# Wider exp tiles and single score and output banks in a planned attention kernel

The change gives ScalarE's exp three PSUM banks at a time instead of two, pays for them with one of VectorE's two score banks and one of the two output banks, shortens VectorE's chains from ten cells to six, and lets the steps of two chains mix.

## The chip, the cores and the metric

The kernel runs on one core of a Trainium2 chip. The metric is device time in microseconds, median of several executions. An execution can fall in a slower state, seen by a lower clock granted to TensorE.

TensorE does the matmuls, ScalarE and VectorE work on their results, and GpSimd does some of the arithmetic beside them. PSUM is the memory that TensorE writes to; this program uses it as eight banks, each of which holds one block of scores or of outputs. SBUF is the core's working memory.

## The reference

```python
batch, n_q_heads, n_kv_heads, seq, head_dim = (8, 8, 2, 1024, 64)
...
scores = scale * np.matmul(q_group, k_group.transpose(0, 1, 3, 2))
scores_max = np.max(scores, axis=-1, keepdims=True)
attn = np.exp(scores - scores_max)
attn = attn / (np.sum(attn, axis=-1, keepdims=True) + 1e-08)
output[:, q_start:q_end, :, :] = np.matmul(attn, v_group)
```

There are 64 heads. Each head is cut into two halves of queries, so there are 128 jobs, and each job has eight cells. A cell is a 128x512 block of scores: 128 keys by 512 queries.

## The kernel before

For each cell TensorE makes a score block in a PSUM bank (one matmul), an exp is taken of it, and TensorE multiplies the result with V (four small matmuls). After eight cells VectorE normalises the job's output. The exp is taken in one of two ways. ScalarE does two cells at a time from a two-bank tile. VectorE converts single cells from banks of their own ("p1", a conversion to an integer that is nearly the bits of the exponential) and then repairs ten of them at a time by a chain: a mask, a linear factor on GpSimd, a product and a sum.

What makes this kernel special is that the order of all this is fixed before launch. A Python function, the planner, walks through the program with assumed durations, always takes the operation that can start first, and writes down a list. Every engine then executes its part of the list in order. In the code, `pe` and `dve` are the times at which TensorE and VectorE come free, `ready` holds the times at which exps are done, `obank_free` the times at which the output banks come free, and `at` is the earliest start of an operation. "qk" is a score matmul, "pv" the output matmuls of a cell, "norm" a normalisation. The parts that matter here:

```python
A_CELLS, D_BANKS, O_BANKS = (2, 2), 2, 2
GROUP, PARTS = 10, 2
# ... in the planner's loop:
        for i, s in enumerate(open_jobs):
            for c in rem[s]:
                at = max(pe, FIRST_PV, ready.get(s * nkc + c, INF))
                if at < INF:
                    best = min(best or (INF,), (at, 3 + i, "pv", (s, c)))
        if len(open_jobs) < O_BANKS and next_job < nj:
            at = min(ready.get(next_job * nkc + c, INF) for c in range(nkc))
            at = max(pe, FIRST_PV, min(obank_free), at)
            if at < INF:
                best = min(best or (INF,), (at, 3 + len(open_jobs), "open", next_job))
# ... cut
        elif kind == "open":
            o = first_free(obank_free)
            obank[arg] = o
            obank_free[o] = INF
            open_jobs.append(arg)
# ... cut
        elif kind == "pv":
            # ... cut
            pe = t + PV
        elif kind == "norm":
            # ... cut
            dve = t + NORM
            obank_free[obank[s]] = dve + FROM_DVE
```

And what the list drives:

```python
    def output_mms(s, cell, opens, closes, bk):
        if opens:
            ops_of[s] = obanks[bk].tile([128, NQS, E1], FP32, name=f"ops{bk}")
        for qs in range(NQS):
            nc.tensor.matmul(ops_of[s][:, qs, :], ...)   # cut
    def normalise(s):
        o = ops_of.pop(s)
        nc.vector.reciprocal(out=rec, in_=o[:, :, D])
        nc.vector.tensor_tensor(out=stage[(b, h)][:, :, side, :], in0=o[:, :, 0:D],
            in1=rec.unsqueeze(2).to_broadcast([128, NQS, D]), op=ALU.mult)
```

The softmax here doesn't subtract the row's maximum and nothing guards it: scores larger than these inputs give would overflow.

Of the kernel before, what the change touches and what calls it, by code (L numbers as in the profile page):

```python
# [11 lines left out]

CURVE_A, CURVE_B = 0.32988085, -0.33401025

A_CELLS, D_BANKS, O_BANKS = (2, 2), 2, 2
GROUP, PARTS = 10, 2
CHAIN = ("and", "line", "prod", "add")
ON_POOL = ("line",)

# [6 lines left out]
def make_plan(nj, nkc):  # L26
# [6 lines left out]

    QK, PV, P1, NORM = 0.216, 0.1225, 0.603, 0.555
    EXP = (0.05, 0.4268)
    FOUR, TWO, POOL_ONE = (0.20, 0.133), (0.16, 0.27), (0.25, 0.43)
    COST = {"and": FOUR, "line": POOL_ONE, "prod": TWO, "add": TWO}
    FROM_PE, FROM_PV, FROM_ACT, FROM_DVE, FROM_POOL = 0.21, 0.16, 0.165, 0.10, 0.15
    LIVE_A, LIVE_D, PENDING, PER_JOB, LEAD, RAMP, AHEAD, FIRST_PV = 28, 5, 16, 2, 6, 6, 0.04, 2.0
    INF = 1e9  # L40
    FIRST_TURN, FIRST_LOAD, EACH_LOAD = 3.3, 4.5, 4.2
    ops = []
    pe = act = dve = 0.0
    a_free, bank, obank_free = [0.0] * len(A_CELLS), [0.0] * D_BANKS, [0.0] * O_BANKS
    todo = [list(range(nkc)) for _ in range(nj)]
    taken = [0] * nj
# [19 lines left out]
    while normed < nj:  # L66
# [3 lines left out]
        lead = min(LEAD, job_a // RAMP)  # L70
        job_d = max(job_d, job_a + lead)
        while job_d < nj and (
            taken[job_d] >= PER_JOB or not todo[job_d]
        ):
            job_d += 1
        if job_a < nj:
# [7 lines left out]
        if job_d < nj and job_d <= job_a + lead + 1 and pending < PENDING:  # L84
            if cur or live["D"] < LIVE_D:
                t = max(pe, min(bank), loaded(job_d))
                if t < INF:
                    best = min(best or (INF,), (t, 2, "qk", 1, t))
        for i, s in enumerate(open_jobs):
            for c in rem[s]:  # L90
                at = max(pe, FIRST_PV, ready.get(s * nkc + c, INF))
# [2 lines left out]
        if len(open_jobs) < O_BANKS and next_job < nj:  # L94
            at = min(ready.get(next_job * nkc + c, INF) for c in range(nkc))
            at = max(pe, FIRST_PV, min(obank_free), at)
            if at < INF:
                best = min(best or (INF,), (at, 3 + len(open_jobs), "open", next_job))
        for q, p, kind in ((normq, 0, "norm"), (p1q, 1, "p1"), (chainq, 2, "chain")):
            if q:  # L100
                at = q[0][0]
                if kind != "chain" or CHAIN[q[0][3]] not in ON_POOL:
                    at = max(dve, at)
                best = min(best or (INF,), (at, p, kind, 0))
        if cur and job_d >= nj and not p1q:
            best = min(best or (INF,), (dve, 9, "flush", 0))
        t, _, kind, arg = best[:4]
        if kind == "qk":
            t = best[4]
            pe = t + QK  # L110
            j = job_d if arg else job_a
            cell = j * nkc + todo[j].pop(0)
            if not arg:
                if open_a is None:
                    slot = first_free(a_free)
                    a_id += 1
                    live["A"] += 1
                    open_a = {"slot": slot, "t": a_free[slot], "cells": []}
                    a_free[slot] = INF
                o = open_a  # L120
                ops.append((t, "qk", cell, "A", a_id, o["slot"], len(o["cells"])))
                o["cells"].append(cell)
                home[cell] = ("A", a_id)
                if len(o["cells"]) == A_CELLS[o["slot"]] or not any(todo[job_a:]):
                    act = max(act, pe + FROM_PE)
                    ops.append((act, "exp", a_id, tuple(o["cells"])))
                    act += EXP[0] + EXP[1] * len(o["cells"])
                    a_free[o["slot"]] = act + FROM_ACT
                    uses[("A", a_id)] = len(o["cells"])
                    for x in o["cells"]:  # L130
                        ready[x] = act + FROM_ACT
                    open_a = None
            else:
                taken[j] += 1
                k = first_free(bank)
                bank[k] = INF
                pending += 1
                ops.append((t, "qk", cell, "D", k, 0, 0))
                p1q.append((pe + FROM_PE, cell, k))
# [5 lines that stand above are left out]
            rem[arg] = list(range(nkc))  # L145
            next_job += 1
        elif kind == "pv":
            s, c = arg
            cell = s * nkc + c
            opens = len(rem[s]) == nkc  # L150
            rem[s].remove(c)
            done = not rem[s]
            ops.append((t, "pv", s, cell, opens, done, obank[s]))
            pe = t + PV
            h = home[cell]
            uses[h] -= 1
            if not uses[h]:
                live[h[0]] -= 1
            if done:
                open_jobs.remove(s)  # L160
                normq.append((pe + FROM_PV, s))
        elif kind == "norm":
            s = normq.pop(0)[1]
            ops.append((t, "norm", s))
            dve = t + NORM
            obank_free[obank[s]] = dve + FROM_DVE
            normed += 1
        elif kind == "p1":
            _, cell, k = p1q.pop(0)
            if not cur:  # L170
                d_id += 1
                live["D"] += 1
            ops.append((t, "p1", cell, k, d_id, len(cur)))
            dve = t + P1
            bank[k] = dve + FROM_DVE
            cur.append(cell)
            home[cell] = ("D", d_id)
            if len(cur) == GROUP:
                chainq.append((dve, d_id, cur, 0))
                cur = []  # L180
        elif kind == "flush":
            chainq.append((dve, d_id, cur, 0))
            cur = []
        else:
            _, g, cells, step = chainq.pop(0)
            ops.append((t, "chain", g, len(cells), CHAIN[step]))
            name = CHAIN[step]
            fixed, each = COST[name.rstrip("0123456789")]
            end = t + fixed + each * len(cells[part(name, len(cells))])
            dve = end if name not in ON_POOL else dve  # L190
            if step + 1 < len(CHAIN):
                at = end
                if (name in ON_POOL) != (CHAIN[step + 1] in ON_POOL):
                    at += FROM_POOL if name in ON_POOL else FROM_DVE
                chainq.insert(0, (at, g, cells, step + 1))
            else:
                pending -= len(cells)
                uses[("D", g)] = len(cells)
                for x in cells:
                    ready[x] = dve + FROM_DVE  # L200
# [4 lines left out]
def kernel(  # L205
# [27 lines left out]
    PIECE = 512  # L233
    WARM = 30
    CAST_GAP = 3.0
    P_TILES = 28
    POOL_DMA = 1.0
    OBSERVE = 8
    scale = 1.0 / math.sqrt(D)
    bits_scale = 128.0 * scale * math.log2(math.e)  # L240
    bits_bias = 128.0 * 127.0
# [30 lines left out]
            for i in range(n)  # L272
        ]

    apools, dbanks, obanks = psum_pools("aps", 2), psum_pools("dps", 2), psum_pools("ops", 2)

    p_ring = const_pool.tile([128, P_TILES, 2, QBS], BF16)
    blank = const_pool.tile([128, 128], BF16)
    nc.vector.memset(blank, 1.0)  # L279
    ident = const_pool.tile([128, 128], BF16)  # L280
# [75 lines left out]
    def first_loads():  # L356
# [5 lines left out]

        hk = first_pool.tile([128, NHC, 3, D], BF16, name="hk")

        tk = [
            dbanks[0].tile([128, HALF], BF16, name="dps0"),
            apools[1].tile([128, HALF], BF16, name="aps1"),
        ]
        lo, hi = slice(0, D), slice(D, 2 * D)

        def turn_k(w, half, bank):
# [21 lines left out]
        for two in range(2):  # L393
            place_v(0, 0, two)

        warm = obanks[1].tile([128, 128], FP32, name="ops1")

        def keep_warm(n):
            for _ in range(n):
# [1 line left out]
            return mm.ins  # L401

        hq = first_pool.tile([128, NHC, 2 * D], BF16, name="hq")
        tq = [
            dbanks[1].tile([128, HALF], BF16, name="dps1"),
            obanks[0].tile([128, HALF], BF16, name="ops0"),
        ]
        qT[(0, 0)] = qT_pool.tile([128, HALF], BF16, name="qT")
        last_score[0] = keep_warm(WARM)
        for n, half in enumerate(halves):  # L410
# [15 lines left out]
            else:  # L426
                nc.vector.tensor_copy(out=qT[(0, 0)][:, cols], in_=tq[n][:, cols])  # L427
                nc.scalar.copy(out=ksets[0][lo, 0, 0, :HALF][:, cols], in_=tk[n][lo, cols])
        nc.scalar.copy(out=qT[(0, 0)][:, : HALF // 2], in_=tq[0][:, : HALF // 2])
        turn_k(1, slice(0, NHC), 0)  # L430
        last_score[0] = keep_warm(4)
        put_k(0, 1, slice(0, NHC), 0)
        nc.gpsimd.dma_start(out=ksets[0][hi, 0, 1, :], in_=ksets[0][lo, 0, 0, :])  # L433

    p_of = {}
    psum = {}
# [6 lines left out]
    def score(cell, kind, n, slot, col):  # L443
        b, h, side = jobs[cell // NKC]
        c = cell % NKC
        if kind == "A":
            if col == 0:
                psum[("A", n)] = apools[slot].tile([128, 2, QBS], FP32, name=f"aps{slot}")
            dst = psum[("A", n)][:, col, :]
        else:  # L450
            dst = psum[cell] = dbanks[n].tile([128, QBS], FP32, name=f"dps{n}")
# [8 lines left out]
    def exps(n, cells):  # L460
# [4 lines left out]
        )  # L465

        exp_ins.append(act.ins)
        if n >= P_TILES and n % OBSERVE == 0:
            seen = exp_ins[n - P_TILES + OBSERVE - 1]
            tc.add_manual_dep(act.ins, seen.name, SYNC, reason="ring")  # L470
        for col, cell in enumerate(cells):
# [15 lines left out]
    def exp_curve(g, m, step):  # L487
# [4 lines left out]
            temps[g] = z, y  # L492
        cells = part(step, m)
        pd, z, y = groups[g][:, cells], temps[g][0][:, cells], temps[g][1][:, cells]
        if step.startswith("and"):
            eng.tensor_scalar(  # L496
                out=z, in0=pd, scalar1=0x7F, scalar2=None, op0=ALU.bitwise_and
            )
# [136 lines left out]
```

## Time and profile before

| | before |
|---|---|
| time, median of 3 runs | 386.97 us |
| span of the profile | 384.9 us |
| ScalarE busy | 375.1 us, 97% |
| TensorE busy | 368.1 us, 96% (matmul records overlap) |
| VectorE busy | 350.1 us, 91% |
| exps | 406 of two cells |
| VectorE's cells | 212 of 1024 |

Records of one engine overlap: an exp's record is 1100 ns long on average, but the next one starts 918 ns after it. So work is best counted in pitches, the differences of start times. The lines themselves stand in the prediction; in them PEld is TensorE's loading of weights, DVE is VectorE, ACT is ScalarE and POOL is GpSimd.

### The profile page before, as it was taken

The page shows a single profiled execution, that of the slowest core. Times are in us where ns is not written, and L with a number is a line of the kernel's source. Part 1 is how long each engine was busy: PE and PEld are TensorE (multiplying, and loading weights), DVE is VectorE, ACT ScalarE, POOL GpSimd, SP SyncE. Part 2 cuts the span into 40 slices and gives each one's busy share as a digit, 9 for nine tenths or more (in the row PEclk, how much of TensorE's full clock was granted, in tenths as well). Part 3 has the DMA queues.
Part 4 walks back from the last instruction along what each step waited for, and adds up shares of the span by engine and source line. Part 5 has one row for each costly group of instructions (what it writes and reads, how often), then busy time and mean ns, then how long its engine had stood idle before and what let it go on. Part 6 is the DMA issues. An engine that isn't in the chain of part 4 may idle for free.

```text
span 384.9 us, 12057 instructions
## 1 busy us (share of the span) xinstructions
PE 368.1 (96%) x5172; PEld 234.5 (61%) x5172; DVE 350.1 (91%) x544; ACT 375.1 (97%) x411; POOL 165.3 (43%) x147
## 2 busy tenths in 40 slices
PE   8879999999999999999999999999999999999985
PEld 6425565656666666666666565666566566666654
DVE  4879999999999999999999999999999999999692
ACT  5999999999999999999999999999999999999994
POOL 5394571716246171625535252535445261531410
PEclk9999999999999999999999999999999999999998
DMA  8888979597859769595865949486584756621213
GB/s 137 152 130 141 141 138 173 113 129 148 128 111 134 132 109 141 123 138 85 151 123 126 125 90 169 74 150 113 119 143 109 111 100 113 109 70 29 71 43 83
DMA packets 102422, 45.49 MB, mean 118 GB/s; under 512 B 63776, under 2 KB 100896, under 8 KB 101120
## 3 DMA queue, kind: packets, MB, share of 16 engines
q1 hardware_dynamic: 82096, 31.21, 37.5%
q0 software_dynamic: 19728, 13.25, 29.8%
q8 instruction: 40, 0.66, 0.8%
q10 hardware_dynamic: 544, 0.26, 0.2%
q14 instruction: 14, 0.11, 0.1%
HBM read 25.17 MB, written 27.00 MB: 136 GB/s over the span
## 4 chain that ended last, share of the span: by engine, by line
ACT 94%; PE 2%; DMA 1%; issue 1%; DVE 0%; SPq 0%; POOLq 0%
ACT p_ring L463 94%; PE ops L522 1%; PE aps L452 1%; DMA fk<-in_k_dram 1%; DMA kset<-kset 1%; SPq L389 0%; DVE ost L538 0%; ACT hk L411 0%; DVE kset L382 0%; DVE qT L427 0%; PE aps L373 0%; DVE rec L535 0%; PE ops L419 0%; PE ops L400 0%; POOLq L433 0%
## 5 line engine op out<-in xcount | busy, mean ns | idle before, releaser
L463 ACT ACTIVATE p_ring<-aps 128x1024 bf16<-128x1024 f32 x406 | 372.4, 1100 | 1.2 <-PE aps L452 1.2
L452 PE MATMUL aps<-qT,kset 128*128 128x512 bf16 x812 | 240.6, 378 | 11.4 <-ACT p_ring L463 8.8
L522 PEld LDWEIGHTS <-p_ring 128*128 128x128 bf16 x3248 | 137.5, 97 | 60.4 <-ACT p_ring L463 0.2
L522 PE MATMUL ops<-vset,p_ring 128*128 128x65 bf16 x3248 | 150.8, 194 | 0.1
L477 DVE TENSOR_SCALAR pd<-dps 128x512 uint16<-128x512 f32 x212 | 138.0, 682 | 13.2 <-PE dps L452 12.3
L500 POOL TENSOR_SCALAR y<-z 128x5120 f16<-128x5120 uint16 (+1 forms) x22 | 94.6, 4301 | 82.7 <-DVE rec L535 45.0
L452 PEld LDWEIGHTS <-kset 128*128 128x128 bf16 x1024 | 82.6, 97 | 58.8 <-issue 26.7
L314 POOL DMA_DIRECT2D scr_q<-in_q_dram x63 | 34.7, 551 | 99.0 <-PE aps L452 47.6
L452 PE MATMUL dps<-qT,kset 128*128 128x512 bf16 x212 | 73.4, 378 | 0.0
L511 DVE TENSOR_TENSOR pd<-pd,y 128x5120 uint16<-128x5120 uint16 (+1 forms) x22 | 59.8, 2719 | 0.1
L509 DVE TENSOR_TENSOR y<-z,y 128x5120 f16<-128x5120 uint16 (+1 forms) x22 | 59.8, 2718 | 0.0
L538 DVE TENSOR_TENSOR ost<-ops,rec 128x256 f32<-128x256 f32 x128 | 54.3, 424 | 4.4
L522 PEld LDWEIGHTS <-pd 128*128 128x128 bf16 x848 | 41.3, 98 | 25.6 <-DVE pd L511 3.6
L522 PE MATMUL ops<-vset,pd 128*128 128x65 bf16 x848 | 48.4, 194 | 0.0
L496 DVE TENSOR_SCALAR z<-pd 128x5120 uint16<-128x5120 uint16 (+1 forms) x22 | 31.7, 1443 | 0.6
L535 DVE RECIPROCAL rec<-ops 128x4 f32<-128x4 f32 x128 | 22.5, 176 | 9.8 <-PE ops L522 8.8
L347 POOL DMA_DIRECT2D vset<-in_v_dram x32 | 24.9, 782 | 0.0
L314 POOL DMA_DIRECT2D scr_k<-in_k_dram x15 | 7.8, 521 | 24.1 <-PE aps L452 16.7
L400 PE MATMUL ops<-blank 128*128 128x128 bf16 x40 | 4.4, 286 | 1.1 <-DVE blank L279 1.1
L400 PEld LDWEIGHTS <-blank 128*128 128x128 bf16 x40 | 3.8, 135 | 1.1 <-DVE blank L279 1.1
L354 POOL DMA_DIRECT2D kset<-kset x6 | 3.2, 537 | 0.0
L411 ACT ACT_TABLE_LOAD x1 | 1.3, 1283 | 1.8 <-issue 1.8
(23 smaller groups left out, 8.7 us busy)
## 6 DMA issues: line engine op xcount, KB each, us to landing
out_dram<-ost SPq DMA_DIRECT2D x63, 256.0 KB, 2.9
scr_q<-in_q_dram POOLq DMA_DIRECT2D x63, 128.0 KB, 3.6
kset<-kT SPq DMA_DIRECT2D x60, 64.0 KB, 3.1
vset<-in_v_dram POOLq DMA_DIRECT2D x32, 64.0 KB, 4.0
scr_k<-in_k_dram POOLq DMA_DIRECT2D x15, 128.0 KB, 3.2
qT<-scr_q SPq DMA_TRANSPOSE x63, 4.0
kset<-kset POOLq DMA_DIRECT2D x7, 128.0 KB, 4.0
fq<-in_q_dram ACTq DMA_DIRECT2D x2, 128.0 KB, 3.2
```

Of the source, the lines that this page charges most:

```text
L314: dma = nc.gpsimd.dma_start(out=scr.rearrange("(p f) -> p f", f=1024), in_=src.rearrange("(p s) d -> p (s d)", s=1024 // D),)
L347: nc.gpsimd.dma_start(out=vsets[b % 2][:, g, two * NHC : (two + 1) * NHC, 0:D], in_=v[b, g].rearrange("(c p two) d -> two p c d", p=128, t ...
L452: last_score[0] = nc.tensor.matmul(dst, lhsT=ksets[b % 2][:, h // HPG, side, c * 128 : (c + 1) * 128], rhs=qT[(b, h)], start=True, stop=Tr ...
L463: act = nc.scalar.activation(out=pt[:, 0:m], in_=psum.pop(("A", n))[:, 0:m], func=AF.Exp, scale=scale)
L477: nc.vector.tensor_scalar(out=groups[g][:, slot], in0=psum.pop(cell), scalar1=bits_scale, scalar2=bits_bias, op0=ALU.mult, op1=ALU.add,)
L496: eng.tensor_scalar(out=z, in0=pd, scalar1=0x7F, scalar2=None, op0=ALU.bitwise_and)
L500: eng.tensor_scalar(out=y, in0=z, scalar1=CURVE_A / 128.0, scalar2=CURVE_B, op0=ALU.mult, op1=ALU.add,)
L509: eng.tensor_tensor(out=y, in0=z, in1=y, op=ALU.mult)
L511: eng.tensor_tensor(out=pd, in0=pd, in1=y, op=ALU.add)
L522: nc.tensor.matmul(ops_of[s][:, qs, :], lhsT=p_of[cell][:, qs * 128 : (qs + 1) * 128], rhs=vsets[b % 2][:, h // HPG, c, :], start=opens an ...
L535: nc.vector.reciprocal(out=rec, in_=o[:, :, D])
L538: nc.vector.tensor_tensor(out=stage[(b, h)][:, :, side, :], in0=o[:, :, 0:D], in1=rec.unsqueeze(2).to_broadcast([128, NQS, D]), op=ALU.mult,)
```

## The change

The intent: an exp of 1536 elements pays the fixed cost of an instruction once for three cells. The eight banks become 3 + 3 for ScalarE, one for VectorE's scores and one for outputs. Shorter chains finish sooner; the planner now keeps GpSimd's linear factor and VectorE's chain steps apart in time. The core of the diff:

```diff
-A_CELLS, D_BANKS, O_BANKS = (2, 2), 2, 2
-GROUP, PARTS = 10, 2
+A_CELLS, D_BANKS, O_BANKS = (3, 3), 1, 1
+GROUP, PARTS = 6, 2
...
-    FOUR, TWO, POOL_ONE = (0.20, 0.133), (0.16, 0.27), (0.25, 0.43)
+    FOUR, TWO, POOL_ONE = (0.09, 0.133), (0.05, 0.27), (0.25, 0.43)
...
-    LIVE_A, LIVE_D, PENDING, PER_JOB, LEAD, RAMP, AHEAD, FIRST_PV = 28, 5, 16, 2, 6, 6, 0.04, 2.0
+    LIVE_A, LIVE_D, PENDING, PER_JOB, LEAD, RAMP, AHEAD, FIRST_PV = 18, 5, 12, 2, 6, 6, 0, 2.0
...
+        for i, (at, _, _, step) in enumerate(chainq):
+            if CHAIN[step] in ON_POOL:
+                at = max(at, pool, two_end)
+            else:
+                at = max(at, dve, pool)
+            best = min(best or (INF,), (at, 2 + i, "chain", i))
...
-    P_TILES = 28
+    P_TILES = 18
...
-    OBSERVE = 8
+    OBSERVE = 16
...
+        nc.scalar.dma_start(
+            out=ksets[0][hi, 0, 1, :HALF], in_=ksets[0][lo, 0, 0, :HALF]
+        )
```

More of the change, by code (lines that the diff above doesn't have):

```diff
@@ L35, in make_plan @@
     EXP = (0.05, 0.4268)
-    FOUR, TWO, POOL_ONE = (0.20, 0.133), (0.16, 0.27), (0.25, 0.43)
+    FOUR, TWO, POOL_ONE = (0.09, 0.133), (0.05, 0.27), (0.25, 0.43)
     COST = {"and": FOUR, "line": POOL_ONE, "prod": TWO, "add": TWO}
     FROM_PE, FROM_PV, FROM_ACT, FROM_DVE, FROM_POOL = 0.21, 0.16, 0.165, 0.10, 0.15
-    LIVE_A, LIVE_D, PENDING, PER_JOB, LEAD, RAMP, AHEAD, FIRST_PV = 28, 5, 16, 2, 6, 6, 0.04, 2.0
+    LIVE_A, LIVE_D, PENDING, PER_JOB, LEAD, RAMP, AHEAD, FIRST_PV = 18, 5, 12, 2, 6, 6, 0, 2.0
     INF = 1e9
-    FIRST_TURN, FIRST_LOAD, EACH_LOAD = 3.3, 4.5, 4.2
+    AHEAD_D, EXTRA, LAST = 0.05, 0, 6
+    FIRST_TURN, FIRST_LOAD, EACH_LOAD = 2.4, 4.5, 4.2
     ops = []
-    pe = act = dve = 0.0
+    pe = act = dve = pool = two_end = 0.0
     a_free, bank, obank_free = [0.0] * len(A_CELLS), [0.0] * D_BANKS, [0.0] * O_BANKS
@@ L72, in make_plan @@
         while job_d < nj and (
-            taken[job_d] >= PER_JOB or not todo[job_d]
+            taken[job_d] >= PER_JOB + EXTRA * (job_d >= nj - LAST)
+            or not todo[job_d]
         ):
@@ L87, in make_plan @@
                 if t < INF:
-                    best = min(best or (INF,), (t, 2, "qk", 1, t))
+                    best = min(best or (INF,), (t - AHEAD_D, 2, "qk", 1, t))
         for i, s in enumerate(open_jobs):
@@ L98, in make_plan @@
                 best = min(best or (INF,), (at, 3 + len(open_jobs), "open", next_job))
-        for q, p, kind in ((normq, 0, "norm"), (p1q, 1, "p1"), (chainq, 2, "chain")):
+        for q, p, kind in ((normq, 0, "norm"), (p1q, 1, "p1")):
             if q:
-                at = q[0][0]
-                if kind != "chain" or CHAIN[q[0][3]] not in ON_POOL:
-                    at = max(dve, at)
-                best = min(best or (INF,), (at, p, kind, 0))
+                best = min(best or (INF,), (max(dve, q[0][0]), p, kind, 0))
+        for i, (at, _, _, step) in enumerate(chainq):
[4 more added lines that the diff above has]
+            best = min(best or (INF,), (at, 2 + i, "chain", i))
         if cur and job_d >= nj and not p1q:
@@ L184, in make_plan @@
         else:
-            _, g, cells, step = chainq.pop(0)
+            _, g, cells, step = chainq.pop(arg)
             ops.append((t, "chain", g, len(cells), CHAIN[step]))
@@ L189, in make_plan @@
             end = t + fixed + each * len(cells[part(name, len(cells))])
-            dve = end if name not in ON_POOL else dve
+            if name in ON_POOL:
+                pool = end
+            else:
+                dve = two_end = end
             if step + 1 < len(CHAIN):
@@ L194, in make_plan @@
                     at += FROM_POOL if name in ON_POOL else FROM_DVE
-                chainq.insert(0, (at, g, cells, step + 1))
+                chainq.insert(arg, (at, g, cells, step + 1))
             else:
@@ L273, in psum_pools @@
         ]
-    apools, dbanks, obanks = psum_pools("aps", 2), psum_pools("dps", 2), psum_pools("ops", 2)
-    p_ring = const_pool.tile([128, P_TILES, 2, QBS], BF16)
+    apools = psum_pools("aps", len(A_CELLS))
+    dbanks, obanks = psum_pools("dps", D_BANKS), psum_pools("ops", O_BANKS)
+    p_ring = const_pool.tile([128, P_TILES, max(A_CELLS), QBS], BF16)
     blank = const_pool.tile([128, 128], BF16)
@@ L363, in first_loads @@
         hk = first_pool.tile([128, NHC, 3, D], BF16, name="hk")
-        tk = [
-            dbanks[0].tile([128, HALF], BF16, name="dps0"),
-            apools[1].tile([128, HALF], BF16, name="aps1"),
-        ]
+        spare = apools[1].tile([128, A_CELLS[1], 2 * QBS], BF16, name="aps1")
+        tk = [dbanks[0].tile([128, HALF], BF16, name="dps0"), spare[:, 0, :HALF]]
         lo, hi = slice(0, D), slice(D, 2 * D)
@@ L394, in first_loads @@
             place_v(0, 0, two)
-        warm = obanks[1].tile([128, 128], FP32, name="ops1")
+        warm = apools[0].tile([128, 128], FP32, name="aps0")
         def keep_warm(n):
@@ L403, in first_loads @@
         hq = first_pool.tile([128, NHC, 2 * D], BF16, name="hq")
-        tq = [
-            dbanks[1].tile([128, HALF], BF16, name="dps1"),
-            obanks[0].tile([128, HALF], BF16, name="ops0"),
-        ]
+        tq = [spare[:, 1, :HALF], obanks[0].tile([128, HALF], BF16, name="ops0")]
         qT[(0, 0)] = qT_pool.tile([128, HALF], BF16, name="qT")
@@ L432, in first_loads @@
         put_k(0, 1, slice(0, NHC), 0)
-        nc.gpsimd.dma_start(out=ksets[0][hi, 0, 1, :], in_=ksets[0][lo, 0, 0, :])
+        nc.gpsimd.dma_start(
+            out=ksets[0][hi, 0, 1, HALF:], in_=ksets[0][lo, 0, 0, HALF:]
+        )
     p_of = {}
@@ L447, in score @@
             if col == 0:
-                psum[("A", n)] = apools[slot].tile([128, 2, QBS], FP32, name=f"aps{slot}")
+                psum[("A", n)] = apools[slot].tile(
+                    [128, A_CELLS[slot], QBS], FP32, name=f"aps{slot}"
+                )
             dst = psum[("A", n)][:, col, :]
@@ L467, in exps @@
         exp_ins.append(act.ins)
-        if n >= P_TILES and n % OBSERVE == 0:
+        if n >= P_TILES and (n - P_TILES) % OBSERVE == 0:
             seen = exp_ins[n - P_TILES + OBSERVE - 1]
@@ L494, in exp_curve @@
         pd, z, y = groups[g][:, cells], temps[g][0][:, cells], temps[g][1][:, cells]
-        if step.startswith("and"):
+        if cells.start == cells.stop:
+            pass
+        elif step.startswith("and"):
             eng.tensor_scalar(
```

## The prediction

> **What bounds the kernel now.** I read the page's engine table first, then the chain that ended last, then the groups of instructions by form, then the waits.
>
> ```profile
> PE 368.1 (96%) x5172; PEld 234.5 (61%) x5172; DVE 350.1 (91%) x544; ACT 375.1 (97%) x411; POOL 165.3 (43%) x147
> ...
> ACT 94%; PE 2%; DMA 1%; issue 1%; DVE 0%; SPq 0%; POOLq 0%
> ```
>
> ScalarE is busy 97% of the 384.9 us span, and 94% of the chain that ended last is its exp line. So a gain must come out of the sum of the exps, or out of the ends. The chain in order of time shows the rhythm:
>
> ```profile
> 6.63 2.48 DMA kset<-kset
> 9.15 0.62 PE aps L452 x2
> 9.80 22.80 ACT p_ring L463 x25
> ...
> 43.64 7.29 ACT p_ring L463 x8
> 50.97 7.31 ACT p_ring L463 x8
> ```
>
> Columns: start, length, what. Eight exps start every 7.33 us (50.97 - 43.64), 0.916 us each. The first exp starts at 6.47 us, a hole of 0.6 us follows at 9.1 us (the DMA that copies K to the other partitions), the last exp ends at 379.3 us, and 5.6 us of output work follow.
>
> ```profile
> L463 ACT ACTIVATE p_ring<-aps 128x1024 bf16<-128x1024 f32 x406 | 372.4, 1100 | 1.2 <-PE aps L452 1.2
> L477 DVE TENSOR_SCALAR pd<-dps 128x512 uint16<-128x512 f32 x212 | 138.0, 682 | 13.2 <-PE dps L452 12.3
> L500 POOL TENSOR_SCALAR y<-z 128x5120 f16<-128x5120 uint16 x21 | 93.6, 4456 | 75.6 <-DVE rec L535 45.0 <-DVE z L496 30.4
> L511 DVE TENSOR_TENSOR pd<-pd,y 128x5120 uint16<-128x5120 uint16 x21 | 59.1, 2815 | 0.1
> L496 DVE TENSOR_SCALAR z<-pd 128x5120 uint16<-128x5120 uint16 x21 | 31.3, 1491 | 0.6
> ```
>
> Of 1024 cells (a 128x512 block of scores) ScalarE takes 812, in 406 pairs, and VectorE 212, in chains of ten. ScalarE idles 1.2 us in all: its supply of scores is perfect. TensorE and VectorE are close behind.
>
> ```profile
> DVE pd L477 <- PE dps L452: 12.3, 25, 2.0
> PE aps L452 <- ACT p_ring L463: 8.8, 30, 0.3
> DVE rec L535 <- PE ops L522: 8.8, 16, 1.5
> ```
>
> Columns: total us, times, longest. With two banks for VectorE's scores and two for outputs these handshakes cost little. The change takes one of each away.
>
> **What the Trainium skill says.** (1) "ScalarE: Activation LUTs", section What ACT_TABLE_LOAD costs: an ACTIVATE with immediate operands takes 186 ns + 0.833 ns per element and back-to-back ones overlap by about 93 ns. For 1024 elements that is a pitch of 946 ns. The trace agrees in form, not in size: the differences of the exps' start times have a floor of 903 and a mean of 918 ns, so 50 ns are fixed and some 15 are waits. I use the trace. (2) "Advanced Engine Details and Errata", section VectorE Performance Modes, says that GpSimd instructions and VectorE's two-port instructions block each other. Here the masking, product and sum are such VectorE work by their pitch of 0.26 and 0.52 ns per element, and no run yet shows the block itself. The new planner forbids their overlap with the linear factor on GpSimd. (3) "Perfetto Trace Analysis", section Matmuls, wants independent matmul groups to rotate through PSUM banks so that one's evacuation overlaps the next's matmuls; the change goes against it in two places. In the trace, counting from an output group's first matmul to the end of its normalisation, both output banks are held at once for 178 us of 374.
>
> **The change part by part.**
>
> *Exp tiles of three banks.* Removes a third of the fixed costs. Pitch for 1536 elements: 50 + 1536 x 0.833 = 1330 ns floor; with 6 ns of waits (the added self-wait comes every 16 exps, not every 8) I take 1336, so 445 ns per cell against 459. For the same 812 cells: 271 x 1.336 = 362 against 406 x 0.918 = 373. That is 11 us, on the path.
>
> *Supply of scores.* A pair needs two matmuls of 215 ns (their pitch in the trace) inside one exp of 903; a triple needs 645 inside 1330. From records of single instructions: an exp ends 0.12 to 0.25 us after the next one starts, the first matmul into its banks starts 0.05 us later, and an exp starts 0.414 us after its last matmul started. So 0.2 + 0.05 + 0.215 + 0.414 = 0.88 of 0.903 us for a pair, 0.2 + 0.05 + 0.43 + 0.414 = 1.09 of 1.33 for a triple: slack grows from next to nothing to 0.24 us. No loss here.
>
> *VectorE's share.* Pitches from the trace's start times: score conversion 597 ns, normalisation 210 + 341 = 551, masking of ten cells 1408, product and sum 2731 each. The latter fit 75 + 0.260 and 64 + 0.521 ns per element. A chain of six is then 875 + 2 x 1664 = 4203 ns, or 0.70 us per cell against 0.69. Work per VectorE cell: 0.597 + 0.70 = 1.30 us; normalisations 128 x 0.551 = 70.5 us. Now VectorE does 127 + 70.5 + 146 = 343 us, 92% of 374. With the same 92 to 94% of about 366 us it can take (340 - 70.5) / 1.30 = 207. One score bank pulls down: a conversion's record ends 83 ns after the next instruction may start (680 - 597), the matmul into its bank comes at best 82 ns later, and the next conversion 415 ns after that: 0.58 us in which VectorE must do something else. Shorter chain steps (1.66 instead of 2.73 us) and mixing push up. I take 208 cells, with 200 to 215 plausible. Then 816 cells, 272 exps, 272 x 1.336 = 363.4 us. Three cells more or fewer are one exp, 1.3 us.
>
> *Start.* The first exp needs a third matmul, +0.2 us; the earlier K copy on ScalarE's queue removes the 0.6 us hole. First exp at 6.7 us.
>
> *End.* With one output bank each of the last jobs must be multiplied (32 x 30 ns = 0.97 us) and normalised (0.16 + 0.55 + 0.1, say 0.8) one after the other, where two banks overlap them: the reciprocals now come 0.98 us apart at the end, then about 1.8. Three jobs were open after the last exp started: +2.4 us, so a tail of 8 us.
>
> *Sum.* 6.7 + 363.4 + 8 = 378.1 us of span; the measured time lies 2.1 us above the span (386.97 against 384.9): 380.2. With 212 cells, the old count, two exps go: 377.5. I put the centre at 379.5.
>
> **The rivals.**
>
> *One output bank makes TensorE the bound.* TensorE issues 1024 x 0.215 + 4096 x 0.0302 = 344 us, and idles 29 us between its first and last work now. In the trace the reciprocal starts 0.66 us after an output group's last matmul on average (median 0.33, at worst 2.7, when a chain step stands in the way) and normalisation takes 0.63. With steps of 1.66 us I estimate 0.45 + 0.63 + 0.1 = 1.2 us in which no output matmul can go, 128 times: 150 us. This leaves 215 us for 124 us of output matmuls, so about 130 of the 220 us of score matmuls would have to fall into those gaps; at their even rate of 0.6 only 90 do. Short by up to 40 us. For it: the arithmetic, and 178 us of double holding. Against it: 18 tiles of finished exps let outputs lag by some eight jobs without stopping ScalarE; score matmuls can cluster in the gaps; and the plan, made before launch, models the one bank and was retuned around it. If it bites in full, 395 us or more; partly, as a long tail of jobs at 1.8 us each, 384 to 390.
>
> *The single score bank starves VectorE.* If each chain of six loses 0.5 us, 35 chains lose 17 us, VectorE takes 13 cells fewer (195), ScalarE 4.4 exps more: 386 us, "same". For it: 12.3 us of such waits even with two banks. Against: 128 normalisations and 105 chain steps exist to fill some 208 gaps.
>
> *All fits.* If chains mix so well that VectorE takes 216 to 220 cells, 268 exps: 268 x 1.334 = 357.5, span 372 and time 374, or 372 with a short tail. For it: chains half as long put fewer cells in waiting, and the start of VectorE's first outputs comes earlier (the first normalisation is at 30 us now).
>
> *A hidden stall in order.* All queues are static. One late normalisation stops TensorE at its head, behind which scores for ScalarE wait. The kernel before had spare banks to swallow this; I add 1 to 3 us to the high side.
>
> **Range and chances.** The ScalarE sum alone gives 374 to 383; output-bank trouble adds a skew upward. Range 371 to 391. Faster by over 2% means under 379.2, almost my centre. That all constants around the banks were retuned speaks for a plan that closes; the output bank's arithmetic speaks against. Faster 0.47, within 2% 0.43, slower 0.10.
>
> **What would show it right or wrong.** Right: about 272 exps of 128x1536 with a pitch near 1336 ns and ScalarE idle under 5 us; first exp at 6.7 us without a hole at 9 us; VectorE conversions near 208; chain steps near 0.95 and 1.75 us long; reciprocals 1.8 us apart at the end and a tail near 8 us. Wrong: ScalarE idle of 10 us or more waiting for TensorE's scores (the output bank or static order is then the bound), conversions below 200 (the score bank starves VectorE), a tail above 12 us (lagging outputs), or a pitch above 1350 (a cost of wide exps that the pairs do not show).

## The result and the profile after

The changed kernel takes 397.67 us (median of 4 runs, 397.59 to 398.04) against 386.99 us of the kernel before on the same chip. The ratio is 1.0278, with a 95% interval of 1.026 to 1.0296. The change is slower by 2.8%, and the time lies outside the range that was predicted.

The page of the changed kernel, its engine table and its chain by engine:

```profile
PE 375.3 (95%) x5172; PEld 222.6 (56%) x5172; DVE 343.2 (87%) x567; ACT 379.0 (96%) x280; POOL 164.4 (42%) x159
...
DVE 46%; PE 33%; ACT 18%; issue 2%
```

No engine is busy for a larger share of the span than before, yet the span grew by 10.9 us. ScalarE's share of the chain fell from 94% to 18%: the end is now set by a path that goes round VectorE, TensorE and ScalarE. Pieces of that chain in order of time (start, length, what):

```profile
7.26 24.49 ACT p_ring L475 x18
36.01 15.01 ACT p_ring L475 x11
64.82 1.66 DVE pd L525
73.91 1.66 DVE y L523
76.72 1.67 DVE pd L525
```

The hole at 9 us is gone, as intended. From about 60 us on the chain passes through VectorE's sums and products every few microseconds. The groups by form that answer to those of before:

```profile
L475 ACT ACTIVATE p_ring<-aps 128x1536 bf16<-128x1536 f32 x275 | 376.3, 1461 | 9.1 <-PE aps L464 2.6
L489 DVE TENSOR_SCALAR pd<-dps 128x512 uint16<-128x512 f32 x199 | 136.6, 686 | 28.1 <-PE dps L464 24.8
L514 POOL TENSOR_SCALAR y<-z 128x3072 f16<-128x3072 uint16 x33 | 90.6, 2745 | 79.9 <-DVE z L510 79.7
L525 DVE TENSOR_TENSOR pd<-pd,y 128x3072 uint16<-128x3072 uint16 x33 | 57.7, 1749 | 0.0
```

VectorE took 199 cells, so there are 275 exps. Their start times have a floor of 1330 ns, just what was worked out, but they do not keep to it. I subtract the floor from every pitch and add up what is left: 17.8 us in the changed kernel, 6.0 us before. Of the 274 pitches 45 are 240 to 270 ns too long, for the most part two in every eight exps. The floors themselves sum to nearly the same, 275 x 1.330 = 365.8 us against 406 x 0.903 = 366.6 us. The waits (total us, times, longest) name the place:

```profile
PEld L536 <- DVE ost L552: 61.7, 120, 0.9
DVE pd L489 <- PE dps L464: 24.8, 43, 1.1
DVE rec L549 <- PE ops L536: 10.9, 10, 2.0
PE aps L464 <- ACT p_ring L475: 3.5, 13, 0.5
```

The first line is new. At 120 of 128 jobs the weight load idles, half a microsecond on average, before the first weights of an output matmul, until VectorE's multiplication (tile ost) has emptied the one output bank. The line of the kernel before was:

```profile
PEld L522 <- DVE ost L538: 0.2, 1, 0.2
```

The weight load runs ahead of the matmuls, so they lose less than it idles: the first output matmul of a job starts 0.18 us later on average than the usual pitch after the matmul before it. The timeline shows one such place (start, length, engine, line, operation, and in brackets the idle time before it and what ended it):

```profile
186.19 0.81 PE L464 MATMUL aps<-qT,kset 128*128 128x512 bf16 x3
186.45 0.18 DVE L549 RECIPROCAL rec<-ops 128x4 f32<-128x4 f32 x1
186.66 0.42 DVE L552 TENSOR_TENSOR ost<-ops,rec 128x256 f32<-128x256 f32 x1
...
187.14 0.18 PEld L536 LDWEIGHTS <-pd 128*128 128x128 bf16 x4 [0.64 <-DVE ost L552]
...
187.28 0.65 PE L536 MATMUL ops<-vset,p_ring 128*128 128x65 bf16 x16
...
187.77 0.59 PE L464 MATMUL aps<-qT,kset 128*128 128x512 bf16 x2
188.20 0.38 PE L464 MATMUL dps<-qT,kset 128*128 128x512 bf16 x1
188.41 0.38 PE L464 MATMUL aps<-qT,kset 128*128 128x512 bf16 x1
```

TensorE issues the three scores of one exp, the last at 186.62, then stands until 187.14, 0.31 us longer than a score's pitch of 0.215. The five output cells that follow (20 matmuls) come late, the three scores of the next exp behind them come late (187.77 to 188.41, with one of VectorE's between), and the exp that needs them starts at 188.83 us, 1.58 us after the last one instead of 1.33.

How large is this effect in all? The kernel's planner gives a start time for every operation, and the trace a real one, in the same order for all 2048 of TensorE's operations. The difference between the two grows by 17.6 us over the program in the changed kernel; before it grew by 4.5. I summed the jumps of this difference along TensorE's program. In the changed kernel +23.3 us fall on the 128 first output matmuls of a job, +2.6 us on VectorE's scores, -7.9 us (time regained) on the first scores of exps. In the kernel before the first output matmuls have +0.1 us. At the place above the plan has the normalisation start at 173.32 and the next job's first output matmul at 173.69. Only 0.37 us lie between them, though the planner's own durations (0.555 + 0.10) ask for 0.655. The chip took 0.69.

The reason is in the planner's code shown above. The event "open" waits for the bank, but it does not move TensorE's clock, and the "pv" event that follows starts at `max(pe, FIRST_PV, ready)`, in which the bank does not appear. With two banks this is harmless. With one, the plan that looked good (it ends at 367.7 us, against 370.3 for the kernel before) left out this wait: at 85 of the 127 hand-overs it has less than 0.655 us between a normalisation and the next job's first output matmul, and in the trace 84 of those matmuls slip by more than 0.1 us.

### The profile page after: what moved, and what is told of

Read it like the earlier page. It is cut to its first block, busy times and chain, and to the rows that moved or that the text cites. A ratio compares the mean times of both kernels' runs of the same rounds, so it can differ in the third digit from the quotient of the medians.

```text
span 395.8 us, 11944 instructions
## 1 busy us (share of the span) xinstructions
PE 375.3 (95%) x5172; PEld 222.6 (56%) x5172; DVE 343.2 (87%) x567; ACT 379.0 (96%) x280; POOL 164.4 (42%) x159
## 4 chain that ended last, share of the span: by engine, by line
DVE 46%; PE 33%; ACT 18%; issue 2%
ACT p_ring L475 18%; PE ops L536 14%; PE aps L464 13%; DVE pd L489 13%; DVE pd L525 11%; DVE y L523 10%; DVE ost L552 9%; PE dps L464 5%; DVE rec L549 3%; PE aps L408 1%; DVE kset L390 0%; DVE qT L432 0%; PE ops L424 0%; PE aps L381 0%; DVE blank L289 0%
## 5 line engine op out<-in xcount | busy, mean ns | idle before, releaser
L475 ACT ACTIVATE p_ring<-aps 128x1536 bf16<-128x1536 f32 x275 | 376.3, 1461 | 9.1 <-PE aps L464 2.6
L464 PE MATMUL aps<-qT,kset 128*128 128x512 bf16 x825 | 244.8, 378 | 4.4 <-ACT p_ring L475 3.5
L489 DVE TENSOR_SCALAR pd<-dps 128x512 uint16<-128x512 f32 x199 | 136.6, 686 | 28.1 <-PE dps L464 24.8
L536 PEld LDWEIGHTS <-p_ring 128*128 128x128 bf16 x3300 | 128.7, 97 | 37.5 <-DVE ost L552 5.1
L536 PE MATMUL ops<-vset,p_ring 128*128 128x65 bf16 x3300 | 145.6, 194 | 0.7 <-DVE ost L552 0.4
L514 POOL TENSOR_SCALAR y<-z 128x3072 f16<-128x3072 uint16 (+1 forms) x34 | 92.7, 2725 | 80.1 <-DVE z L510 80.0
L536 PEld LDWEIGHTS <-pd 128*128 128x128 bf16 x796 | 32.6, 97 | 60.0 <-DVE ost L552 56.6
L523 DVE TENSOR_TENSOR y<-z,y 128x3072 f16<-128x3072 uint16 (+1 forms) x34 | 58.1, 1710 | 1.2 <-POOL y L514 1.2
L525 DVE TENSOR_TENSOR pd<-pd,y 128x3072 uint16<-128x3072 uint16 (+1 forms) x34 | 58.1, 1710 | 0.0
L510 DVE TENSOR_SCALAR z<-pd 128x3072 uint16<-128x3072 uint16 (+1 forms) x34 | 32.9, 967 | 1.0
L549 DVE RECIPROCAL rec<-ops 128x4 f32<-128x4 f32 x128 | 22.6, 177 | 11.4 <-PE ops L536 10.9
L408 PE MATMUL aps<-blank 128*128 128x128 bf16 x40 | 4.5, 290 | 1.1 <-DVE blank L289 1.1
```

The source lines that it names most:

```text
L464: last_score[0] = nc.tensor.matmul(dst, lhsT=ksets[b % 2][:, h // HPG, side, c * 128 : (c + 1) * 128], rhs=qT[(b, h)], start=True, stop=Tr ...
L475: act = nc.scalar.activation(out=pt[:, 0:m], in_=psum.pop(("A", n))[:, 0:m], func=AF.Exp, scale=scale)
L489: nc.vector.tensor_scalar(out=groups[g][:, slot], in0=psum.pop(cell), scalar1=bits_scale, scalar2=bits_bias, op0=ALU.mult, op1=ALU.add,)
L510: eng.tensor_scalar(out=z, in0=pd, scalar1=0x7F, scalar2=None, op0=ALU.bitwise_and)
L514: eng.tensor_scalar(out=y, in0=z, scalar1=CURVE_A / 128.0, scalar2=CURVE_B, op0=ALU.mult, op1=ALU.add,)
L523: eng.tensor_tensor(out=y, in0=z, in1=y, op=ALU.mult)
```

## The experiments

Theory A: the hold of the single output bank, a wait that the plan does not contain, delays the scores of the exps and makes the 12 us of new waits. Theory B: the single score bank, or VectorE's load as such, sets the pace, and the wait at the output bank is only where it shows. The first nine kernels keep the changed kernel's static order and move VectorE work in or out of the time in which a bank is held. The kernel before ran beside every one, at medians of 386.88 to 387.19 us, so runs of different rounds are compared directly.

### Holding the output bank longer, and the same work elsewhere

o_slow puts an instruction of 128 elements in front of the normalisation, reading the output bank. o_late puts one of the same size after it, reading SBUF.

```diff
 # o_slow, before the reciprocal
+        nc.vector.tensor_scalar(out=idle, in0=o[:, 0:2, 0:D], scalar1=1.0, scalar2=0.0, ...)
 # o_late, after the multiplication
+        nc.vector.tensor_scalar(out=idle, in0=rec[:, 0:2].unsqueeze(2).to_broadcast([128, 2, D]), ...)
```

> Changed kernel, same static order; one extra VectorE instruction of 128 elements reads the output bank before each normalisation, so the single output bank is held about 0.2 us longer, 128 times. Theory A (TensorE stands at the first output matmul of a job until the one output bank is free; this is what delays the scores of the exps): the 120 waits of the weight load on the normalisation grow from 61.7 us by about 0.2 us each to 85, and the time rises by 15 to 25 us over 397.7, to 412 to 422. Theory B (the single score bank and VectorE's load bind): the same as o_late within 3 us. The result stays correct.

> The same extra VectorE instruction, but after the normalisation and reading SBUF, so VectorE's load grows the same 25 us and the output bank's release does not move. Theory A: clearly less than o_slow, 398 to 408, because the bank is released as before and only the next conversions and normalisations come later. Theory B (VectorE's load binds): as slow as o_slow.

o_slow: 421.34 us (421.33 to 421.44), as theory A says. The weight load's wait grew as expected:

```profile
PEld L536 <- DVE ost L556: 86.9, 124, 1.1
```

o_late: 450.98 us, which neither theory says. The group of the added instruction in o_late explains it (busy us, mean ns, idle before):

```profile
L559 DVE TENSOR_SCALAR idle<-rec 128x128 f32<-128x128 f32 x128 | 80.0, 625 | 0.0
```

The median is 217 ns, the longest 2430. 36 of the 128 took over 400 ns, and 32 of these began inside GpSimd's linear factor; they ended a median 83 ns after its end. Reading SBUF, this instruction had to wait for GpSimd. The Trainium skill, "SBUF — State Buffer", section SBUF: two separate sides, has an exclusive pair of ports that VectorE and GpSimd share, and this run agrees. In o_slow, where the instruction reads PSUM, 32 of the 128 began inside the linear factor too, and none took over 292 ns. So o_late tested a third thing and says nothing on A or B. I made it again with an instruction that shows no such waits:

```diff
 # o_late2, after the multiplication
+        nc.vector.reciprocal(out=idle, in_=rec.unsqueeze(2).to_broadcast([128, NQS, 4]))
```

> o_late again, because its extra instruction got stuck behind GpSimd's linear factor (36 of 128 took up to 2.4 us): the extra one is now a reciprocal of 16 elements per partition, about 0.2 us[...]. Theory A (the hold of the output bank is what counts): 398 to 410 us, clearly under o_slow's 421.3. Theory B (VectorE's load counts, wherever it lies): 415 to 423.

o_late2: 404.48 us (404.19 to 404.58); the 128 reciprocals took 241 to 245 ns each, also the 33 that began inside GpSimd's linear factor. The wait is near that of the changed kernel:

```profile
PEld L536 <- DVE ost L552: 66.9, 119, 0.9
```

The doses are not quite the same: the pitch of the added instruction is 0.20 us in o_slow and 0.16 us in o_late2, so the added loads are 25 and 20 us (VectorE's busy time grew by 22.9 and 11.9 us). o_slow cost 23.7 us and o_late2 6.8 us. Load that also lengthens the hold costs nearly its full length; load outside the hold costs a third of its pitches, or somewhat over half of its busy time. Theory A's ranges hold in both.

### Holding the output bank shorter

o_quick2 multiplies only a quarter of each output (and sends it four times, so the result is wrong), and then does the same filling reciprocal. The inputs are so small (0.1 times normal numbers) that all queries of a head get nearly the same output. o_light leaves the filling out. o_quick was a first form, filled with an instruction that reads SBUF like o_late's.

```diff
 # o_quick2 and o_light
-            in0=o[:, :, 0:D],
-            in1=rec.unsqueeze(2).to_broadcast([128, NQS, D]),
+            in0=o[:, 0:1, 0:D],
+            in1=rec[:, 0:1].unsqueeze(2).to_broadcast([128, 1, D]),
 # o_quick2 only
+        nc.vector.reciprocal(out=idle, in_=rec.unsqueeze(2).to_broadcast([128, NQS, 4]))
```

> Wrong result on purpose: only a quarter of the outputs is multiplied out of the output bank; a second VectorE instruction that reads SBUF writes the other three quarters, so the bank is released about 0.2 us sooner while VectorE's load even grows a little. Same static order. Theory A: the waits of the weight load on the normalisation fall from 61.7 to about 40 us, the exps' pitch excess falls from 17.8 us to 8 to 12, the time to 387 to 392. Theory B: no faster than 397.7.

> Wrong result on purpose: a quarter of the outputs is multiplied and sent four times, so the output bank is released about 0.2 us sooner; the same reciprocal of 16 elements follows, so VectorE's load stays what it was. Same static order. Theory A: the slip at each job's first output matmul falls from 23 us in all to 8 or less, time 382 to 390. Theory B: 395 to 400.

> Wrong result on purpose: as o_quick2 without the filling reciprocal, so VectorE's load falls by about 25 us as well. Theory A: at most 4 us under o_quick2, 380 to 388. Theory B: all of the gain comes here and none in o_quick2.

o_quick: 441.72 us, its result wrong. Its filling instruction waited for GpSimd as in o_late (32 of 128, up to 2.7 us), so its time says nothing. o_quick2: 385.26 us (385.11 to 385.34), 12.4 us less than the changed kernel. VectorE's load is about 5 us less by pitches, its busy time 10.4 us less (332.8 against 343.2); at the rate of o_late2, 6.8 us for 11.9 us of busy time, this could be worth 6 us at most, so load alone does not make the gain. o_light: 383.88 us; another 20 us of load taken from VectorE (128 x 0.16) are worth 1.4 us. In o_quick2 the exps' excess over their floor is 5.3 us, a little under that of the kernel before (6.0), and the jumps at first output matmuls sum to 5.8 us instead of 23.3. The wait lines of o_quick2:

```profile
PEld L536 <- DVE ost L552: 30.2, 83, 0.7
DVE pd L489 <- PE dps L464: 25.4, 64, 1.0
```

The wait at the output bank is halved. The wait of VectorE for its scores, which theory B would have as the cause, is what it was (24.8 us). Theory A is shown: 0.2 us less hold per job removes all the new waits of ScalarE.

### Holding the score bank longer

d_slow and d_late do the same at the score bank: an added instruction in front of each of the 199 conversions that reads the bank, or after it from SBUF. d_late2 takes the reciprocal.

```diff
 # d_slow, before the conversion
+        nc.vector.tensor_scalar(out=idle, in0=psum[cell][:, 0 : 2 * D]..., scalar1=1.0, scalar2=0.0, ...)
 # d_late, after the conversion: the same from a tile of ones in SBUF
 # d_late2, after the conversion
+        nc.vector.reciprocal(out=idle, in_=ones4.unsqueeze(2).to_broadcast([128, NQS, 4]))
```

> One extra VectorE instruction of 128 elements reads the score bank before each of the 199 conversions: the single score bank is held about 0.2 us longer and VectorE's load grows by about 39 us. Theory A: no more than d_late does. Theory B (score bank): 10 us or more slower than d_late.

> The same extra instruction after each conversion, reading SBUF: the score bank is released as before, VectorE's load grows by 39 us. Theory A: about the same time as d_slow. Theory B: at least 10 us faster than d_slow. In both theories it is slower than 397.7, since VectorE has only some 50 us of idle time left.

> Changed kernel, same order, a reciprocal of 16 elements (about 0.2 us) after each of the 199 conversions, so that VectorE's load grows by about 39 us and the score bank is released as before; d_slow put the same load in front of the release and took 424.2. If the hold of the score bank matters by itself: 415 or less. If only VectorE's load and its effect on the normalisations count: 420 to 428.

d_slow: 424.15 us. d_late: three of its four executions were slow, its profile too, and the fast one took 481.41 us; it is spoiled by the same waits for GpSimd (36 of 199 instructions over 400 ns, up to 2.5 us) and not used. d_late2: 407.58 us (407.46 to 407.7). It lies in the range of 415 or less that was written for a hold that matters by itself. How much of the 16.6 us between the two is the hold stays open: the added loads differ by 8 us by pitches (39 and 32 us), but VectorE's busy time by 14.9 us (376.3 and 361.4). What shows the hold is the jumps: on VectorE's scores they sum to 19.9 us in d_slow, against 2.6 in the changed kernel (d_late2's trace lacks some matmul records, so its jumps were not summed). So my expectation under theory A, that d_slow would cost no more than the same load elsewhere, was wrong: lengthening this hold costs time too. But in the changed kernel as it stands the plan contains the score bank's wait (2.6 us of jumps are left), so it costs mainly cells in the plan and little waiting on the chip.

### Charging the wait in the plan

honest changes only the planner. It adds the bank to the start of output matmuls.

```diff
-                at = max(pe, FIRST_PV, ready.get(s * nkc + c, INF))
+                at = max(pe, FIRST_PV, o_at[s], ready.get(s * nkc + c, INF))
...
             obank[arg] = o
+            o_at[arg] = obank_free[o]
```

> Only the planner is changed: it charges the wait for the output bank to the first output matmul of a job, which it left out before. Its plan for the same banks then ends at 445 us instead of 368. Theory A (the planner's missing wait is all that separates plan and chip): the chip follows the honest plan with the offset of 10 us or so that the kernel before shows, 450 to 460 us. If the honest plan is wrong and the chip would not feel the bank, it runs near 390.

honest: 461.37 us (461.17 to 464.29). The plan ends at 444.6, and the chip follows it: the difference of planned and real start grows from 6.0 to 10.4 us over the exps, as it does in the kernel before (5.8 to 10.4), and the jumps at first output matmuls sum to 1.1 us. That is a little over the range I wrote, because I had set the offset of time against plan too low: for the kernel before it is 386.97 - 370.3 = 16.7 us, and here 16.8. So once the wait is charged, a plan for these banks lies as far under the chip as other plans do. The honest plan is much slower than the changed kernel, as I read it because its greedy rule issues scores as soon as it can and leaves none for the time in which the output bank is held; no run tests this. That the faulty plan ordered them better is luck.

honest7 is the best order that a search over the planner's constants found for the same banks with the wait charged (chains of seven, latencies set from the trace, and a few other constants).

> The changed kernel's banks (exps of three, one score bank, one output bank) with the best order that a search over the planner's constants found once the wait for the output bank is charged: chains of seven, plan 388.4 us, VectorE 173 cells, 284 exps. If a good order could hide one output bank, this or something near it would show it. The chip should follow the plan with 8 to 10 us on top: 396 to 400, no better than the changed kernel's 397.7. If the charged wait overstates the bank, under 390.

honest7: 405.21 us (404.76 to 405.5), 16.8 us above its plan of 388.4. My range was again too low by the offset. Of the orders that were searched, none hides one output bank. ScalarE is fed (3.9 us over the floor), but VectorE takes only 173 cells, and 14.5 us of outputs follow the last exp. Other rules than this greedy one were not tried.

### One part alone, from the kernel before

b_o1, b_d1 and b_g6 start from the kernel before and change one thing, planned anew by its old planner. The tiles of the start move where a bank is gone, which is cut here.

```diff
 # b_o1
-A_CELLS, D_BANKS, O_BANKS = (2, 2), 2, 2
+A_CELLS, D_BANKS, O_BANKS = (2, 2), 2, 1
 # b_d1
+A_CELLS, D_BANKS, O_BANKS = (2, 2), 1, 2
 # b_g6
-GROUP, PARTS = 10, 2
+GROUP, PARTS = 6, 2
```

> The kernel before with one output bank instead of two, planned anew by its own planner (plan 397 against 370 us, both without the wait). Theory A: far above its plan plus 10, that is 415 us or more, with large waits on the normalisation. Theory B: near 407 or below.

> The kernel before with one bank for VectorE's scores instead of two, planned anew (plan 384, 183 cells for VectorE instead of 212). Theory A: it follows its plan, 394 to 397 us, ScalarE stays fed (421 exps of two at 0.917 us); the loss is all from the 29 cells that go back to ScalarE. Theory B would add waits on top, over 400.

> The kernel before with chains of six instead of ten, nothing else (planned anew: 381.4 us, VectorE 194 cells, 415 exps). If shorter chains alone cost VectorE cells in a plan of the old kind: 390 to 394, ScalarE still fed. If shorter chains help, as the prediction had it: under 387.

| kernel | plan ends, us | measured, us | difference | VectorE's cells |
|---|---|---|---|---|
| before | 370.3 | 386.97 | 16.7 | 212 |
| b_g6 | 381.4 | 397.78 | 16.4 | 194 |
| b_d1 | 384.0 | 401.58 | 17.6 | 183 |
| b_o1 | 397.2 | 475.08 | 77.9 | 220 |
| changed | 367.7 | 397.67 | 30.0 | 199 |
| honest | 444.6 | 461.37 | 16.8 | 218 |

b_o1 is the strongest case, far over the 415 us of theory A. Its plan misses the same wait, and the chip is 78 us above the plan; the jumps at first output matmuls sum to 72 us. b_d1 is slower than I wrote for either theory's clean case (over 400), but it is 17.6 us above its plan, about as the kernel before; by the corrected offset it follows its plan, and the loss is that of 29 cells that went back to ScalarE. b_g6 is slower than I wrote too (390 to 394), for the same offset. Both show that fewer score banks and shorter chains each take cells from VectorE in this planner. That is a property of its greedy order with these constants, and both kernels keep constants that were tuned for other settings; I do not claim that chains of six must cost this much.

### The new planner on the old banks

pairs9 takes the changed kernel's code with the wait charged, latencies set from the trace, and the old banks: exps of two, two score banks, two output banks, chains of nine. The edit, cut:

```diff
+A_CELLS, D_BANKS, O_BANKS = (2, 2), 2, 2
+GROUP, PARTS = 9, 2
+    LIVE_A, LIVE_D, PENDING, PER_JOB, LEAD, RAMP, AHEAD, FIRST_PV = 28, 5, 16, 2, 7, 6, 0.08, 2.0
+    OBSERVE = 24
```

> The new planner with the wait for the output bank put in and with its latencies set from the trace, on the old banks: exps of two banks, two score banks, two output banks, chains of nine, self-wait every 24 exps. Plan 367.9 us against 370.3 of the kernel before, VectorE 214 cells, 405 exps. Theory A says that a plan without a missing wait is followed by the chip: 382 to 386 us, faster than before by 0.3 to 1.2%. If the mixing of chains or the new planner itself is what costs, it is slower than before.

pairs9: 384.9 us (384.29 to 385.12, 5 runs) against 386.88 us, ratio 0.9947 with an interval of 0.9934 to 0.9959; correct. It beats both kernels, by 0.5% and 3.2%. It is 17.0 us above its plan of 367.9. Its waits:

```profile
PEld L537 <- DVE ost L553: 0.9, 2, 0.5
DVE pd L490 <- PE dps L465: 7.1, 13, 1.1
ACT p_ring L476 <- PE aps L465: 1.5, 2, 1.0
```

With two output banks the wait is gone, and VectorE takes 214 cells. So the mixing of chains and the new planner are not what costs. Exps of three banks alone, with the other banks as they were, were not run: with two score and two output banks they would need ten banks of the eight.

## Why the prediction was wrong

It had the span as 378.1 us by its sum; the span was 395.8, that is 17.7 us more. By its own steps:

- **Exp tiles of three banks.** The size of an exp was right: a floor of 1330 ns was worked out and measured. The 6 ns of waits that the step added were wrong by a factor of ten: 17.8 us over 274 pitches are 65 ns. Against the predicted 1.6 us this is 16.2 us, nearly the whole miss.
- **Supply of scores: "No loss here."** This is the step that failed. It compared three matmuls with one exp as if TensorE could always issue them when the bank came free. TensorE works through its list in order, and what stood in front of the scores was an output matmul that waited for the bank. These first output matmuls slipped by 23.3 us in all, 0.31 us at the place shown, more than the slack of 0.24 us that was worked out without any output matmul in between. Instead of no loss (1.6 us were allowed for) there were 17.8 us of waits in the exps' pitches.
- **The first rival, "One output bank makes TensorE the bound",** named the right cause. It estimated 1.2 us in which no output matmul can go; from the start of the last output matmul to the reciprocal the trace has 0.33 us on average, normalisation 0.64, the hand-back to the next matmul 0.06 (median), so about 1.0. It foresaw "up to 40 us". The case against it was the error: "the plan, made before launch, models the one bank and was retuned around it". The plan did not contain that wait, which the code shows, and I had read the line that frees the bank without following it to the operation that should wait for it.
- **The last rival, "A hidden stall in order",** named the mechanism itself: a late normalisation stops TensorE, behind which scores for ScalarE wait. It was given 1 to 3 us; 11.8 us of new waits were measured.
- **VectorE's share.** 208 cells predicted, 199 measured, below the plausible 200 to 215: three exps more, 4.0 us. The rival on the score bank gave 195 for its case, so this part of it was close; its sign, "conversions below 200", came true by one cell. b_d1 and b_g6 show one score bank and chains of six each lowering the count in plans. Durations of chain steps were right (0.95 and 1.75 us predicted, 0.96 and 1.75 measured).
- **Start.** First exp at 7.26 instead of 6.7 us, 0.6 us late: the new order puts one of VectorE's scores in front. The hole at 9 us did vanish.
- **End.** The tail after the exps was predicted at 8 us; counting the last exp with one pitch it was 5.0 us, 3 us better. The last reciprocals are 2.0 and 1.9 us apart, as predicted (1.8), but fewer jobs were left over.

The parts sum: 16.2 + 4.0 + 0.6 - 3.0 = 17.8, against 17.7. The prediction's own list of signs held "ScalarE idle of 10 us or more waiting for TensorE's scores (the output bank or static order is then the bound)". In substance this came true: 17.8 us by the pitches. The listed idle was only 9.1 us, under the 10 that it asks for, since most of the waits hide under overlapping records. The sign "a pitch above 1350" came true as well (1395 on average), but not for the cause it names, a cost of wide exps: the floor stayed at 1330.

Where did the expected gain go? The wider exps do save: 812 cells would cost 360.0 us of floors instead of 366.6. VectorE's 13 lost cells take back 5.8 us of these 6.6, and the output bank takes 12 us more.

## What to carry to other kernels

Before you trust a static order, follow each buffer's release in the planner to the very operation that must wait for it, and check that the wait moves that engine's clock; time minus plan was 16.4 to 17.6 us for every plan here without the missing wait, and the two that stood out (30.0 and 77.9) had it. An engine that works through a fixed list and waits for one consumer delays all others behind it, so compute slack with what may stand in front in its queue. Giving up the second buffer of a hand-over exposes the hand-over's length each time, less what can be put in its place: here about 1.0 us, 128 times, of which ScalarE felt 12 us.

## What the Trainium skill lacked or had wrong

- "ScalarE: Activation LUTs", section What ACT_TABLE_LOAD costs, does not say whether its figures are for operands in SBUF or in PSUM. As an estimate, those for immediate operands give a pitch of 93 ns + 0.833 ns per element back to back. The runs, which read PSUM, show 50 ns + 0.833: floors of 903 ns for 1024 elements and 1330 ns for 1536.
- The page "VectorE: DVE Perf Modes" gives no duration for the reciprocal. Here one of 4 elements from PSUM takes 177 ns and one of 16 from SBUF 243 ns, and of 128 of the latter (241 to 245 ns) none waited for GpSimd, though 33 began inside its linear factor.
- "PSUM — Partial Sum Buffer", section PSUM bank collisions raise a hardware error, tells to guard banks by semaphores, but the page gives no cost of handing a bank over. Here 0.23 us pass at the least from the start of the last output matmul to the start of VectorE's reciprocal, and 0.06 us from the end of VectorE's multiplication to the start of the next matmul.
